# A fused two-block kernel: every matmul operand moved down by 32 bytes in SBUF

## The chip, the core and the metric

The kernel runs on one NeuronCore of a Trainium2 chip. The metric is the device time of one execution in microseconds; three runs of the kernel before stand behind the median. All arithmetic is in fp32, and nearly all matmuls read their operands as fp32r.

## What is computed

The reference is two residual blocks in sequence on one sequence of 256 tokens with 1024 channels. Cut to its matmuls:

```python
# block 1
proj = rmsnorm(x) @ w_in              # q, k, v, gates of three mixers
mixed = sum(sigmoid(gate_b) * (mixer_b(proj) @ w_branch_b))   # GLA, pooling, block attention
x = x + rmsnorm(mixed @ w_out)
f = (silu(h @ ffn_w_gate) * (h @ ffn_w_up)) @ ffn_w_down      # h = rmsnorm(x)
x = x + rmsnorm(f)
# block 2: the same shape with other mixers (HGRN2, mLSTM, SSD),
# a causal convolution in the FFN and a last rmsnorm
```

All the large products have K = 1024 (or 512, or 2816) and 256 rows. To keep fp32 accuracy each is made of three fp32r products: high part by high part, low part by high part, and high part by low part.

## The kernel before

**Tiles.** The packed weights are cut into 172 pieces of up to 2144 columns. `fetch` (L422 and after) brings a piece from HBM into a raw buffer `wr` on SP's queue, ScalarE rounds it into the high part `wh` (`act`, L283), and VectorE makes the low part `wl` by subtracting (`tt`, L286). There are two raw buffers and three each of `wh` and `wl`, so pieces are loaded and split ahead of the matmuls. Activations that feed matmuls are split in the same way, into `hhi`/`hlo` (the normed input) or into pairs of "big" buffers `b` (tag `b8`, ten of them), which also serve everything else of that size.

**Matmuls.** `three` (L445 and after) issues the products of a piece in order: all K tiles of one of the three combinations, then those of the next. There are two forms. In `proj_cm` the weights are stationary (128 columns of `wh` or `wl`) and the activations move (256 columns): the records `pp<-hhi,wh`, `pp<-hlo,wh`, `pp<-hhi,wl`, `pp<-b,wh` and `pp<-b,wl` with 128x256. In `mm_tm` (`proj_tm`, `out_tiles`, `down_tiles`, `first_tm`) the activations are stationary and the weights move, 512 columns as a rule; 256 in the first pieces of each FFN; 264 and 268 in four odd pieces whose rows in the buffer are 1056 and 1072 bytes long. All matmuls are issued by `mm`, so they share line L297; generators stepped by `tick` put the small matmuls of the mixers between the pieces.

**What lies where in a partition.** The pools are laid one behind the other: `cp` (the small constants and `x`), `wp` (`wr`, `wh`, `wl`), `pd` (a dead tile of 48 floats, 192 bytes), `big`, `hp` (`hhi`, `hlo`), `wk`. The widths of the repeated buffers are padded: `WW` = 2176 floats is 34 times 256 bytes, `BW` = 2112 floats is 33 times 256, and two `wr` of `PW` = 2144 floats are 67 times 256. So all `wh` and `wl` have one address residue modulo 256, and all big buffers and `hhi`/`hlo` have another, 192 higher. K tiles within a buffer lie 1024 or 2048 bytes apart (1056 and 1072 in the odd pieces). In the kernel before, the residues are 32 for `wh`/`wl` and 224 for the big buffers and `hhi`/`hlo`; the two `wr` are at 32 and 160.

**The lines that the change touches.** `setup` (L331 to L347) allocates `cp`'s tiles in this order: `x`, `const`, `vecs`, `wg2`, `mhalf`, `ones`, `sgain`, and last `pad`, 8 floats that nothing reads or writes. `const` holds the identity that the transposes use as the moving operand.

Of the kernel before, what the change touches and what calls it, by code (L numbers as in the profile page):

```python
# [8 lines left out]
F32 = mybir.dt.float32  # L9
# [220 lines left out]
class Prog:  # L230
# [102 lines left out]
    def setup(self):  # L333
        nc, A = self.nc, self.A
        self.x = self.cp.tile([128, 2, D], F32, name="x")
        self.const = self.cp.tile([128, CONST.shape[1]], F32, name="const")
        self.vec = self.cp.tile([128, VEC_N], F32, name="vecs")
        self.wg2 = self.cp.tile([16, 256], F32, name="wg2")
        self.mhalf = self.cp.tile([128, 16], F32, name="mhalf")
        self.warm = self.wk.tile([128, 1024], mybir.dt.bfloat16, tag="junk", name="warm", bufs=1)[:, :128]  # L340
        self.nc.vector.memset(self.warm, 0.0)
        self.nc.vector.memset(self.mhalf, -0.5)
        self.ones = self.cp.tile([128, 128], F32, name="ones")
        self.nc.vector.memset(self.ones, 1.0)
        self.sg = self.cp.tile([128, 16], F32, name="sgain")
        self.ident = self.c("ident")
        self.cp.tile([128, 8], F32, name="pad")  # L347

    def load_first(self):

# [1205 lines left out]
```

## Time and profile before

| | us |
|---|---|
| median of three runs | 1045.87 (1043.8 to 1047.94) |
| the profiled execution | 1044.58 |
| its span, first to last instruction | 1042.8 |
| TensorE busy in the span | 1028.4 (99%) |
| weight loads busy (beside the matmuls) | 963.8 (92%) |
| VectorE busy | 749.1 (72%) |
| ScalarE busy | 602.6 (58%) |

[...]

### The profile page before, as it was taken

How to read it: one execution, taken by the hardware profiler on the slowest of the kernel's cores; microseconds unless marked ns; L12 is line 12 of the kernel's file. 1: busy time of each engine (PE TensorE's matmuls, PEld its weight loads, DVE VectorE, ACT ScalarE, POOL GpSimd, SP SyncE). 2: the span in 40 equal slices, each digit the busy share in tenths (PEclk: the TensorE clock that was granted, in tenths of full speed). 3: DMA queues.
4: the chain of work that ended last, by engine and by line, in shares of the span. 5: the costliest groups of instructions: out<-in, count | busy, mean ns of one | idle time of the engine just before them, and what ended most of it. 6: DMA issues, size and time to landing. Idle time of an engine off the chain costs nothing.

```text
span 1042.8 us, 21285 instructions
## 1 busy us (share of the span) xinstructions
PE 1028.4 (99%) x8748; PEld 963.8 (92%) x8748; DVE 749.1 (72%) x1469; ACT 602.6 (58%) x1262; POOL 31.1 (3%) x53
## 2 busy tenths in 40 slices
PE   8999999999999999999999999999999999999997
PEld 7899999989999988799889899999999989999885
DVE  5767578586555645756888879877776785999753
ACT  6667555466544544744468656754565565767542
POOL 1000000000000000000020000000100000000000
PEclk9999999999999999999999999999999999999999
DMA  8654445555555556355435455455646464555561
GB/s 303 214 202 134 160 160 175 200 195 202 203 170 203 194 182 218 133 201 200 146 131 204 133 186 178 167 189 185 217 162 212 173 221 163 190 192 189 183 212 46
DMA packets 31345, 191.09 MB, mean 183 GB/s; under 512 B 3880, under 2 KB 5216, under 8 KB 10256
## 3 DMA queue, kind: packets, MB, share of 16 engines
q1 hardware_dynamic: 28544, 181.12, 49.9%
q0 software_dynamic: 2128, 7.57, 2.3%
q8 instruction: 68, 1.11, 0.4%
q10 hardware_dynamic: 576, 1.05, 0.3%
q14 instruction: 29, 0.24, 0.1%
HBM read 188.65 MB, written 1.08 MB: 182 GB/s over the span
## 4 chain that ended last, share of the span: by engine, by line
PE 95%; DVE 2%; ACT 1%; issue 1%; DMA 0%; POOL 0%; POOLq 0%; SPq 0%; ACTq 0%
PE pp L297 88%; PE m L297 5%; PE m L548 1%; DMA vecs<-vec 0%; PE m L615 0%; DVE wl L286 0%; DVE b L286 0%; ACT wh L283 0%; PE m L990 0%; PE m L814 0%; DVE k L289 0%; POOL k L567 0%; ACT hhi L283 0%; ACT b L283 0%; PE m L1321 0%
## 5 line engine op out<-in xcount | busy, mean ns | idle before, releaser
L286 DVE TENSOR_TENSOR wl<-wr,wh 128x512 fp32r<-128x512 f32 (+2 forms) x660 | 423.7, 681 | 174.7 <-ACT wh L283 91.1
L283 ACT ACTIVATE wh<-wr 128x512 fp32r<-128x512 f32 (+2 forms) x660 | 373.1, 618 | 281.1 <-PE pp L297 247.9
L297 PE MATMUL pp<-hhi,wh 128*128 128x256 f32 x1440 | 200.1, 280 | 1.1 <-ACT hhi L283 1.1
L297 PE MATMUL pp<-hlo,wh 128*128 128x256 f32 x1440 | 194.2, 277 | 0.0
L297 PE MATMUL pp<-hhi,wl 128*128 128x256 f32 x1440 | 193.8, 277 | 0.0
L297 PEld LDWEIGHTS pp<-hhi,wh 128*128 128x128 f32 x1440 | 179.8, 188 | 4.0 <-ACT hhi L283 2.1
L297 PEld LDWEIGHTS pp<-hlo,wh 128*128 128x128 f32 x1440 | 177.8, 188 | 0.0
L297 PEld LDWEIGHTS pp<-hhi,wl 128*128 128x128 f32 x1440 | 177.7, 188 | 0.0
L297 PE MATMUL pp<-wh,b 128*128 128x512 f32 x512 | 131.6, 397 | 1.7 <-ACT wh L283 1.7
L297 PEld LDWEIGHTS pp<-wh,b 128*128 128x128 f32 x512 | 97.0, 191 | 23.6 <-ACT wh L283 2.0
L297 PE MATMUL pp<-b,wh 128*128 128x256 f32 x576 | 74.6, 279 | 0.0
L289 DVE SCALAR_TENSOR_TENSOR k<-pp,vecs,k 128x255 f32<-128x255 f32 (+1 forms) x148 | 70.2, 478 | 6.1 <-ACT k L283 5.2
L297 PE MATMUL pp<-wl,b 128*128 128x512 f32 x256 | 71.4, 396 | 0.0
L297 PEld LDWEIGHTS pp<-b,wh 128*128 128x128 f32 x576 | 69.5, 188 | 0.1
L297 PEld LDWEIGHTS pp<-wl,b 128*128 128x128 f32 x256 | 48.7, 190 | 10.6
L297 PE MATMUL pp<-wh,hhi 128*128 128x512 f32 (+3 forms) x232 | 52.2, 355 | 0.0
L297 PE MATMUL pp<-wh,hlo 128*128 128x512 f32 (+3 forms) x232 | 50.2, 347 | 0.2 <-issue 0.2
L297 PE MATMUL pp<-wl,hhi 128*128 128x512 f32 (+3 forms) x232 | 50.3, 347 | 0.0
L283 ACT ACTIVATE k<-pp,vecs 128x256 f32<-128x256 f32 x62 | 34.5, 558 | 15.8 <-DVE k L289 11.3
L297 PEld LDWEIGHTS pp<-wh,hlo 128*128 128x128 f32 x232 | 38.0, 188 | 6.0 <-issue 0.3
L283 ACT ACTIVATE k<-k 128x512 f32<-128x512 f32 (+2 forms) x47 | 27.0, 574 | 28.4 <-DVE k L289 23.7
L297 PEld LDWEIGHTS pp<-wl,hhi 128*128 128x128 f32 x232 | 37.9, 188 | 5.6
(178 smaller groups left out, 929.6 us busy)
## 6 DMA issues: line engine op xcount, KB each, us to landing
wr<-w SPq DMA_DIRECT2D x158, 1024.0 KB, 4.8
wr<-w SPq DMA_DIRECT2D x10, 512.0 KB, 4.2
k<-rows POOLq DMA_DIRECT2D x16, 192.0 KB, 3.4
wr<-w SPq DMA_DIRECT2D x10, 256.0 KB, 4.4
wr<-w SPq DMA_DIRECT2D x2, 1072.0 KB, 4.9
wr<-w SPq DMA_DIRECT2D x2, 1056.0 KB, 5.1
b<-gains POOLq DMA_DIRECT2D x2, 1024.0 KB, 6.5
b<-xt SPq DMA_DIRECT2D x8, 128.0 KB, 4.5
```

The lines of the kernel that those rows point to most:

```text
L283: return self.nc.scalar.activation(out=out, in_=in_, func=func, **k)
L286: return self.nc.vector.tensor_tensor(out=out, in0=a, in1=b, op=op)
L289: return self.nc.vector.scalar_tensor_tensor(out=out, in0=a, scalar=s, in1=b, op0=op0, op1=op1)
L297: return self.nc.tensor.matmul(out, lhsT=lhsT, rhs=rhs, start=start, stop=stop)
L548: self.nc.tensor.transpose(ps[:, k], part[:, 128 * k:128 * k + 128], self.ident)
```

## The change

One allocation is dropped, the unused tile `pad` of 32 bytes a partition:

```diff
         self.sg = self.cp.tile([128, 16], F32, name="sgain")
         self.ident = self.c("ident")
-        self.cp.tile([128, 8], F32, name="pad")
```

Everything allocated ahead of it (`x`, `const`, `vecs`, `wg2`, `mhalf`, `ones`, `sgain`) stays where it is. Everything behind it moves down by 32 bytes: the weight buffers go from residue 32 to 0 modulo 256, the big buffers and `hhi`/`hlo` from 224 to 192, the raw buffers from 32 and 160 to 0 and 128, and the work tiles with them. The distance between any two of these stays the same. No instruction is added, removed or reordered.

## Rows read from the trace of the kernel before

**Rows 1.** The page: the span, busy time by engine, and the clock row.

```profile
span 1042.8 us, 21285 instructions
PE 1028.4 (99%) x8748; PEld 963.8 (92%) x8748; DVE 749.1 (72%) x1469; ACT 602.6 (58%) x1262; POOL 31.1 (3%) x53
PEclk9999999999999999999999999999999999999999
```

**Rows 2.** The page: the chain that ended last, by engine.

```profile
PE 95%; DVE 2%; ACT 1%; issue 1%; DMA 0%; POOL 0%; POOLq 0%; SPq 0%; ACTq 0%
```

**Rows 3.** Groups by line and form on TensorE: xcount | busy us, mean ns.

```profile
L297 PE MATMUL pp<-hhi,wh 128*128 128x256 f32 x1440 | 200.1, 280 | 1.1 <-ACT hhi L283 1.1
...
L297 PE MATMUL pp<-b,wh 128*128 128x256 f32 x576 | 74.6, 279 | 0.0
...
L297 PE MATMUL pp<-b,wl 128*128 128x256 f32 x288 | 40.8, 277 | 0.0
```

**Rows 4.** TensorE's timeline, weights stationary, fast: start us, us, what; first and last.

```profile
40.02 1.07 PE L297 MATMUL pp<-hhi,wl 128*128 128x256 f32 x8
...
971.73 1.07 PE L297 MATMUL pp<-hhi,wl 128*128 128x256 f32 x8
...
974.45 1.07 PE L297 MATMUL pp<-hhi,wl 128*128 128x256 f32 x8
```

**Rows 5.** The same view and shape, slow stretches: the first and the last.

```profile
71.28 1.10 PE L297 MATMUL pp<-hlo,wh 128*128 128x256 f32 x8
...
75.05 1.10 PE L297 MATMUL pp<-hhi,wl 128*128 128x256 f32 x8
...
777.47 1.11 PE L297 MATMUL pp<-b,wl 128*128 128x256 f32 x8
```

**Rows 6.** Stretches: PE, PEld, DVE, ACT, POOL busy us, clock, DMA share; two slow, one fast.

```profile
71.30:75.90 4.60, 4.60 (x42) 4.60 (x40) 1.35 (x3) 1.51 (x5) 0.00 (x0) 1.00 0.56 183
110.00:114.90 4.90, 4.90 (x44) 4.90 (x44) 4.13 (x17) 2.58 (x10) 0.00 (x0) 1.00 0.01 3
...
692.30:697.50 5.20, 5.20 (x48) 5.20 (x47) 3.26 (x6) 1.97 (x5) 0.00 (x0) 1.00 0.53 180
```

**Rows 7.** TensorE's timeline: a piece with rows of 1056 bytes, weights moving.

```profile
65.59 1.13 PE L297 MATMUL pp<-wl,hhi 128*128 128x264 f32 x8
66.56 1.13 PE L297 MATMUL pp<-wh,hhi 128*128 128x264 f32 x8
```

**Rows 8.** TensorE's timeline: the first FFN's first pieces, 256 columns moving.

```profile
238.85 1.12 PE L297 MATMUL pp<-b,hlo 128*128 128x256 f32 x8
239.81 2.08 PE L297 MATMUL pp<-b,hhi 128*128 128x256 f32 x16
...
244.81 1.10 PE L297 MATMUL pp<-wh,hlo 128*128 128x256 f32 x8
245.75 1.11 PE L297 MATMUL pp<-wl,hhi 128*128 128x256 f32 x8
```

**Rows 9.** Groups by line and form on TensorE: 512 columns moving, from `wh`, from `b`.

```profile
L297 PE MATMUL pp<-wh,hhi 128*128 128x512 f32 x136 | 38.0, 400 | 0.0
...
L297 PE MATMUL pp<-b,hhi 128*128 128x512 f32 x16 | 4.4, 398 | 0.0
```

**Rows 10.** Groups by line and form on ScalarE and VectorE: the splits.

```profile
L283 ACT ACTIVATE wh<-wr 128x512 fp32r<-128x512 f32 x628 | 358.6, 623 | 260.9 <-PE pp L297 232.2 <-DMA wr<-w 21.2 <-issue 6.1
...
L283 ACT ACTIVATE b<-wr 128x512 fp32r<-128x512 f32 x28 | 15.5, 620 | 7.8 <-DMA wr<-w 7.8
...
L286 DVE TENSOR_TENSOR wl<-wr,wh 128x512 fp32r<-128x512 f32 x628 | 407.5, 687 | 154.8 <-PE pp L297 82.1 <-ACT wh L283 71.2 <-issue 0.4
...
L286 DVE TENSOR_TENSOR b<-wr,b 128x512 fp32r<-128x512 f32 x28 | 17.8, 687 | 6.8 <-ACT b L283 6.8
```

**Rows 11.** Groups by line and form on TensorE: transposes, identity moving.

```profile
L548 PE MATMUL m<-const,b 128*128 128x128 f32 x56 | 7.4, 272 | 0.0
...
L990 PE MATMUL m<-const,k 128*128 128x128 f32 x24 | 4.6, 271 | 0.0
```

## The prediction

> **What bounds the kernel now.** First the busy table and the clock: TensorE is busy 1028.4 of 1042.8 us at the full granted clock throughout [rows 1]. Then the chain that ended last: 95% of it is TensorE [rows 2], and the rest lies mostly at the start and the end. So the time is the sum over 8748 matmuls of what each costs in the stream. Next, which matmuls: 1440 each of `hhi,wh`, `hlo,wh` and `hhi,wl`, 576 of `b,wh` and 288 of `b,wl` have stationary weights and 256 moving columns, 5184 or six in ten [rows 3]; the first row there stands for its three.
>
> Last the timeline, where the finding is. Twenty-four such matmuls go from 971.73 to 974.45, 2.72 us or 113.3 ns each [rows 4]. Elsewhere thirty-two of the same shape on the same kinds of buffer go from 71.28 to 75.05, 3.77 us or 117.8 ns each [rows 5]. Counted from start to start over the whole trace, for steps between two matmuls of this form without a gap, 4042 take 113 to 116 ns (mean 113.4) and 1035 take 117 to 124 (mean 117.9); the first and the last rows of either kind stand in [rows 4, 5]. They aren't mixed: a stretch, usually the 48 matmuls of a piece, keeps one rhythm from its first few matmuls to its end. The rhythm does not follow the other engines: one slow stretch has the DMA engines 56% busy and VectorE 29%, another has DMA at 1% and VectorE at 84%, a fast one lies between with 53% and 63%, all at clock 1.00 and with the weight loads busy all the time [rows 6]. So TensorE is held back by something of its own. Two reads of SBUF run in it at once, the moving operand of one matmul and the weights of the next, and I take it that they collide, in a pattern that depends on their addresses and on how the stretch was entered.
>
> **The trace's own evidence on addresses.** The odd pieces keep the stationary operand at residue 224 while the moving one advances by 32 modulo 256 from one matmul to the next, so eight matmuls visit eight places. Eight take 0.97 us, 121.2 ns each at 264 columns [rows 7]; counted from start to start the mean is 121.0, in a settled cycle of 116 to 126 ns with the same time at the same place each round. [...] Two further pairings stand in the FFN's first pieces: both operands at residue 224, 0.96 us for eight, 120 ns; stationary 224 and moving 32, 0.94 us, 117.5 ns by the row and 118.0 by the count [rows 8]. Of all pairings that whole stretches have, that of the bulk, stationary 32 and moving 224, is the only one with a rhythm near 113.
>
> **The change, part by part.**
> *The 5184 matmuls with stationary weights.* Their operands go to residues 0 and 192, a pair that the trace does not hold. Is it the place or the distance that counts? The distance stays at 192. [...] If the place counts, the expectation is the mean over places, 117.7 [rows 7], not the best: 4042 x (117.7 - 113.4) = 17.4 us more, and 1035 x (117.9 - 117.7) = 0.2 less, together 17 us. Bounds: all at the worst settled pairing, 120 [rows 8], 4042 x 6.6 + 1035 x 2.1 = 28.9 us more; all at the best place seen, 112.7, 4042 x 0.7 + 1035 x 5.2 = 8.2 us less. I take 17, by the row with eight places in steps of the very 32 bytes.
> *The matmuls with 512 moving columns*, 1248 by the count: moving from `wh` at 32 or from `b` at 224 past the same stationary 224, the records last 400 and 398 ns [rows 9]. They hardly see the address; I take 0, bounded by 2 ns either way, 2.5 us.
> *The other forms with 256 to 268 moving columns and stationary activations*, 480 by the count: they already sit at the slow rhythm or above, so 0, bounded by 480 x 5 = 2.4 us, likelier as a gain than as a loss.
> *The transposes*, 174: here alone the distance changes, since the identity stays. The stationary operand lies at 224 in one row and at 32 in the other, 272 against 271 ns [rows 11]: 174 x 1 ns = 0.2 us, nothing.
> *The splits on ScalarE and VectorE* write `wh`/`wl` at residue 32 and `b` at 224 in the same 623 and 620 ns, and in the same 687 and 687 ns [rows 10]. Their addresses cost nothing there, so 0. The cover, if I am wrong, is that ScalarE mostly waits for TensorE, 232.2 us of the 260.9 idle ahead of its splits; 3 ns on 656 splits is 2 us of that, and without the cover it would be 2 us.
> *The loads* into `wr` land at other residues. ScalarE's splits waited only 21.2 us for them in the whole run [rows 10], nearly all behind pieces already split, so a faster landing is worth nothing and a slower one is covered by the buffers ahead; 0, with 0.5 us either way at the start, where the chain isn't on TensorE.
>
> Sum, against the profiled execution: 1044.6 + 17 = 1061.6, so 1062 us. Outside the span lie 1.8 us that don't change. This execution is 1.3 us under the median of the three, inside their spread of 4.1. The measurement can tell 0.5%, 5.2 us, from no change.
>
> **Rivals.**
> *A, the forecast: the place counts and the fast rhythm is lost*, 1062 us. For it: the fast rhythm stands alone among the pairings of whole stretches. [...] Its own range is 1050 (a third of the stretches still fast, -5.8 us, and some 6 us of gain at the other forms and bounds) to 1076 (28.9 + 2.5 over 1044.6).
> *B, only the distance counts*, 1045 us. Where the two reads meet depends on one address less the other if the memory repeats in steps of 32 bytes or less, and a shift of both changes nothing. For it: the weight buffers, which lie 512 apart modulo 1024, and both halves of a piece show the same 113.4, so the pattern does repeat. What can still move is how the stretches fall into the two rhythms: the longest, one in each FFN, are 860 matmuls each, so one of them entered the other way is 860 x 4.5 = 3.9 us. That alone is nearly the spread of the runs. Range 1040 to 1051.
> [...]
> *C, the new places are better*: every stretch finds the fast rhythm or a better one. The slow rhythm disappears, 1035 x 4.5 = 4.7 us, and with the best place seen it is 8.2 us, plus up to 2.4 at the other forms. 1044.6 - 6.5, the middle of the first two, is 1038 us, range 1034 to 1040. [...]
> *D, the change doesn't do what it says*, because the allocator puts the buffers elsewhere: the pools are laid in order and the tile has no reader, so this is unlikely; 1045 us as B.
>
> **How the numbers follow.** A 0.45, B 0.31, C 0.22, D 0.02. [...] The predicted time is A's, 1062. The range leaves out half of C (below 1038) and the top of A (above 1075), about 0.16: 1038 to 1075. Faster by over 0.5%: C less a little, plus a little of B, 0.22. Slower: A less a little that stays within 5 us, plus a little of B, 0.44. Within: 0.34.
>
> **What the new profile would show.** If A: in the timeline of the stationary-weight stretches eight take 0.94 to 0.96 us where most now take 0.907, the recorded mean of these groups rises from 277 to about 281 ns, and the FFN stretches of 860 are slow throughout; VectorE's and ScalarE's splits stay at 687 and 623. If B: the same two steps, 0.907 and 0.945, in shares near four to one. If C: a single step of 0.907 or less. The prediction is wrong if the 512-column stream moves by more than 2 ns a matmul, or if the splits' durations change; then the reading that only TensorE's own two reads see the address fails.

## The result

| | before | after |
|---|---|---|
| median of four runs, us | 1044.84 (1043.36 to 1047.94) | 1054.27 (1051.73 to 1055.52) |
| profiled execution, us | 1044.58 | 1054.15 |
| its span, us | 1042.8 | 1052.3 |
| ratio, with its 95% interval | | 1.0085 (1.0067 to 1.0103) |

The change makes the kernel 0.85% slower, 9.4 us. The page of the kernel after, the lines that answer to [rows 1]:

```profile
span 1052.3 us, 21285 instructions
PE 1036.2 (98%) x8748; PEld 972.5 (92%) x8748; DVE 748.1 (71%) x1469; ACT 602.0 (57%) x1262; POOL 31.1 (3%) x53
PEclk9999999999999999999999999999999999999999
```

TensorE has the same 8748 matmuls and is busy 7.8 us longer; VectorE and ScalarE need no more than before. Where, the chain that ended last tells, in order of time: start us, us, what. First three of its longest pieces in the kernel before, then the same three after:

```profile
263.38 151.51 PE pp L297 x1098
...
785.79 62.83 PE pp L297 x468
...
877.58 151.51 PE pp L297 x1098
```

```profile
261.01 155.35 PE pp L297 x1098
...
789.83 64.50 PE pp L297 x468
883.29 155.35 PE pp L297 x1098
```

3.84 + 1.67 + 3.84 = 9.35 us of the 9.5 us by which the spans differ, in three stretches. In each the part that changed is a run of matmuls with stationary weights: 863 steps, from one start to the next, in either FFN, and 383 in eight pieces at the end of block 2's branches (at 785 us). Outside the three, the two executions differ by -2.4 us ahead of the first stretch and by +2.6 between the first and the second, which nearly cancels. That is luck of the two profiles. The first 30 us took longer in this profile of the kernel before than in any other profile here, by 1.1 to 2.5 us. The +2.6 are mostly a wait and a spell of lower clock near 530 and 548 us of the kernel after, which the profile of before does not have there:

```profile
532.29 0.52 PE L297 MATMUL pp<-hlo,wh 128*128 128x256 f32 x3 [1.33 <-issue]
...
547.00:550.40 3.40, 3.40 (x40) 0.53 0.68 219
```

The first line is from the timeline, with an idle time of 1.33 us in square brackets; the second is a stretch, in which the granted clock was 0.53, against 1.00 in the same window of the kernel before. A kernel without the loss has the wait too (1.35 us, with the work tiles put back, below), and a kernel with the loss has no such spell of lower clock there (the unused bytes first, below), so neither is the change's loss.

The timeline of TensorE shows how one of them begins, first before, then after. Columns as in [rows 4]; L990 before and L989 after are the same line, the last two transposes ahead of the first FFN's stretch.

```profile
263.00 0.38 PE L990 MATMUL m<-const,k 128*128 128x128 f32 x2
263.13 1.17 PE L297 MATMUL pp<-hhi,wh 128*128 128x256 f32 x8
264.14 1.07 PE L297 MATMUL pp<-hlo,wh 128*128 128x256 f32 x8
265.05 1.07 PE L297 MATMUL pp<-hhi,wl 128*128 128x256 f32 x8
```

```profile
260.62 0.38 PE L989 MATMUL m<-const,k 128*128 128x128 f32 x2
260.76 1.19 PE L297 MATMUL pp<-hhi,wh 128*128 128x256 f32 x8
261.79 1.11 PE L297 MATMUL pp<-hlo,wh 128*128 128x256 f32 x8
262.73 1.11 PE L297 MATMUL pp<-hhi,wl 128*128 128x256 f32 x8
```

The records of neighbouring matmuls overlap: eight last 1.07 us before and 1.11 after, while the next eight start 0.91 and 0.94 us on. So the time of one is taken here from the starts, the step to the next row divided by eight. Eight matmuls take 0.91 us before and 0.94 after, the very two rhythms of [rows 4] and [rows 5], and the difference is there from the second group of eight on. It lasts to the end of the stretch. The view by stretches, with the matmuls that start in the same 96.8, 43.0 and 97.0 us, before and then after. (The kernel after enters its second and third stretch 3.6 and 5.1 us into these windows, so a few other matmuls are counted there.)

```profile
263.20:360.00 96.80, 96.80 (x856) 1.00 0.55 191
786.00:829.00 43.00, 43.00 (x382) 1.00 0.57 203
878.00:975.00 97.00, 97.00 (x858) 1.00 0.55 188
```

```profile
263.20:360.00 96.80, 96.80 (x824) 1.00 0.54 185
786.00:829.00 43.00, 43.00 (x369) 1.00 0.53 184
878.00:975.00 97.00, 97.00 (x828) 1.00 0.52 180
```

In these windows TensorE is busy all the time, at clock 1.00, and gets through 32, 13 and 30 fewer matmuls.

**No rhythm changed its length.** Counted from the starts, past the first steps of a stretch, the fast rhythm is 113.33 ns and the slow one 117.78 in the long stretches of both kernels, to the hundredth (with the entry, a whole fast FFN stretch has 113.35). What changed is the share over the whole trace: 1035 of 5077 steps are slow before, 3184 of 5066 after. The matmuls outside this form kept their times: 117.9 ns (stationary 224 or 192, moving 32 or 0), 121.0 at 264 columns, 123.9 and 124.1 at 268, 229.2 and 229.2 at 512. So moving all operands by 32 bytes changed nothing where both operands of a matmul moved.

### The profile page after: what moved, and what is told of

It reads as the page before. It is cut to its first block, busy times and chain, and to the rows that moved or that the text cites. A ratio compares the mean times of both kernels' runs of the same rounds, so it can differ in the third digit from the quotient of the medians.

```text
span 1052.3 us, 21285 instructions
## 1 busy us (share of the span) xinstructions
PE 1036.2 (98%) x8748; PEld 972.5 (92%) x8748; DVE 748.1 (71%) x1469; ACT 602.0 (57%) x1262; POOL 31.1 (3%) x53
## 3 DMA queue, kind: packets, MB, share of 16 engines
q8 instruction: 68, 1.11, 0.4%
## 4 chain that ended last, share of the span: by engine, by line
PE 94%; DVE 2%; DMA 1%; ACT 1%; issue 1%; POOL 0%; SPq 0%; POOLq 0%; ACTq 0%
PE pp L297 87%; PE m L297 5%; DMA wr<-w 1%; PE m L547 1%; DMA x<-x 1%; PE m L614 0%; DVE wl L286 0%; DVE b L286 0%; POOL k L566 0%; ACT junk L561 0%; ACT wh L283 0%; PE m L989 0%; PE m L813 0%; DVE k L289 0%; ACT b L283 0%
## 5 line engine op out<-in xcount | busy, mean ns | idle before, releaser
L297 PE MATMUL pp<-hhi,wh 128*128 128x256 f32 x1440 | 203.0, 282 | 1.1 <-ACT hhi L283 1.1
L297 PE MATMUL pp<-hlo,wh 128*128 128x256 f32 x1440 | 198.2, 280 | 1.3 <-issue 1.3
L297 PE MATMUL pp<-hhi,wl 128*128 128x256 f32 x1440 | 197.0, 280 | 0.0
L297 PEld LDWEIGHTS pp<-hhi,wh 128*128 128x128 f32 x1440 | 182.2, 189 | 4.0 <-ACT hhi L283 2.1
L297 PEld LDWEIGHTS pp<-hlo,wh 128*128 128x128 f32 x1440 | 181.4, 189 | 1.5 <-issue 1.4
L297 PEld LDWEIGHTS pp<-hhi,wl 128*128 128x128 f32 x1440 | 180.9, 189 | 0.0
```

The costliest lines, as they stand in the source:

```text
L297: return self.nc.tensor.matmul(out, lhsT=lhsT, rhs=rhs, start=start, stop=stop)
```

## The experiments

After the result the theories were these. **E**: the length of a rhythm is set by the distance of the two operands; which rhythm a stretch falls into is set by how it is entered, that is by what TensorE read just before, and there the identity of the transposes is an operand that did not move. **P**: the place modulo 256 of weights and activations makes the slow rhythm likelier. **X**: the entry falls by chance.

### The kernel before, a second profile

No edit.

> The kernel before, unchanged, profiled a second time. In the first profiles of before and after, each long stretch of matmuls with stationary weights keeps one of two rhythms, 113.3 or 118 ns a matmul; three long stretches (860, 860 and 382 matmuls, entered near 263, 877 and 786 us) are fast before and slow after, and they are worth 9.7 us. Theory E (the entry is set by program and addresses: the transposes just ahead read the identity, which the change did not move): all three are fast again, near 1044 us. Theory X (the entry falls by chance, and the two profiles happened to differ): one or more of the three are slow here, 2 to 10 us more in the span. Theory P (the place of the weights modulo 256 makes the slow rhythm likelier): as E.

Measured: 1043.3 us, span 1041.5. The stretches of 863, 383 and 863 have 113.35, 113.36 and 113.35 ns, as in the first profile. Of the 53 stretches some short ones, and one of 183 steps, fall otherwise than in the first profile, 1277 slow steps against 1035, which is 1.1 us. So chance has a small share and not the three long stretches. The times of all executions say the same: all four of the kernel after took 1051.7 us or more, and none of 17 of the kernel before took more than 1047.7. X falls for these.

### The unused bytes ahead of `x` and `const`

```diff
+        self.cp.tile([128, 8], F32, name="pad")
         self.x = self.cp.tile([128, 2, D], F32, name="x")
         self.const = self.cp.tile([128, CONST.shape[1]], F32, name="const")
...
-        self.cp.tile([128, 8], F32, name="pad")
```

> Before, with the unused 32 bytes allocated ahead of x and const instead of behind them: the weights stay at residue 32 and the big buffers at 224, as before, but the identity moves up by 32, so its distance to everything behind is that of the changed kernel. Theory E (what counts is the distance between the identity and the tiles that the transposes ahead of a stretch turn): the three long stretches are slow, ratio 1.008 to 1.010, about 1054 us. Theory P (the place of the weights and activations modulo 256 counts): as before, ratio 1.000 within 0.2%. Theory X (chance): no fixed answer.

Measured: 1055.93 us, ratio 1.0105 (1.0087 to 1.0123). All three long stretches are slow, 117.78 ns. The entry of the second FFN's, from this kernel's timeline:

```profile
883.34 0.38 PE L990 MATMUL m<-const,k 128*128 128x128 f32 x2
883.48 1.19 PE L297 MATMUL pp<-hhi,wh 128*128 128x256 f32 x8
884.50 1.11 PE L297 MATMUL pp<-hlo,wh 128*128 128x256 f32 x8
885.45 1.10 PE L297 MATMUL pp<-hhi,wl 128*128 128x256 f32 x8
```

Here not one weight or split activation lies elsewhere than before; only `x` and the small constants ahead of them moved. Of these TensorE reads, beside the identity, only `ones` and `wg2`, in eight matmuls that all lie in the first 80 us. The slowdown of the change is there in full, so the place of the weights is not its cause. P falls.

### The identity moved along

The changed kernel, with small tiles put between `x` and `const`, so that the identity goes down by 32 modulo 256 like all the rest.

```diff
         self.x = self.cp.tile([128, 2, D], F32, name="x")
+        self.mhalf = self.cp.tile([128, 16], F32, name="mhalf")
+        self.sg = self.cp.tile([128, 16], F32, name="sgain")
+        self.r0 = [self.cp.tile([128, 1], F32, name=f"r0_{t}") for t in range(2)]
+        self.ml_gain = self.cp.tile([128, 8], F32, name="mlg")
         self.const = self.cp.tile([128, CONST.shape[1]], F32, name="const")
```

> The changed kernel with 224 bytes of small tiles (mhalf, sgain, the two r0 and mlg) allocated between x and const instead of behind, so that the identity too goes down by 32 modulo 256, from 128 to 96, with the weights at 0 and the big buffers at 192. All distances modulo 256 among the operands of the large matmuls and the transposes are those of before. Theory E: the three long stretches are fast, ratio 1.000 within 0.2%, about 1045 us. Theory P: slow as after, 1.008 to 1.010, about 1054 us.

Measured: 1045.15 us, ratio 1.0009 (0.9993 to 1.0025). The three stretches are fast, and with the weights at 0 and the activations at 192 the time of before is back. Timeline at the entry of the stretch of 383:

```profile
782.92 1.04 PE L549 MATMUL m<-const,b 128*128 128x128 f32 x8
783.71 1.17 PE L297 MATMUL pp<-hhi,wh 128*128 128x256 f32 x8
784.72 1.07 PE L297 MATMUL pp<-hlo,wh 128*128 128x256 f32 x8
785.62 1.07 PE L297 MATMUL pp<-hhi,wl 128*128 128x256 f32 x8
```

These two runs and the two kernels make a square: weights at the old or the new place, identity at the old or the new distance. The time follows the distance of the identity in both rows.

### Only the work tiles back

The changed kernel with 32 unused bytes at the head of the work pool, which puts the work tiles, and they alone, back where they were before.

```diff
+        self.wk.tile([128, 8], F32, tag="padk", name="padk", bufs=1)
         self.nc.vector.memset(self.warm, 0.0)
```

> The changed kernel with 32 unused bytes put into the work pool, so that the work tiles alone go back to their places of before (the 256-column ones to residue 160) while weights, big buffers and normed input stay at 0 and 192 and the identity at 128. The transposes that turn a work tile (line 990, just ahead of the two FFN stretches of 860, and line 814) have their distance of before again; those that turn a big buffer (lines 548, 615, 1321, ahead of the stretch of 382 near 786 us and the one of 285 near 182 us) keep that of the changed kernel. Theory E: the two FFN stretches are fast, the stretch of 382 stays slow: 8.0 us less than the changed kernel, about 1046.3, ratio 1.002. Rival P': it is the shift of the FFN's own operands, weights and normed input, that makes their stretches slow: no gain, 1054, ratio 1.009.

Measured: 1043.74 us, ratio 1.0003 (0.9992 to 1.0013). The two FFN stretches are fast, as E said and P' denied. But the stretch of 383 is fast too, which E's account had slow: its last transposes turn a big buffer and kept the distance of the changed kernel. So the last transposes alone don't decide there. The edit moved the work tiles against the big buffers as well, and these meet in the small matmuls of the SSD that run among the pieces just ahead: the five stretches of 48 to 96 matmuls that are entered from such a matmul (716 to 778 us) are slow in both kernels and fast here. The traces show one thing more that differs, the rhythm of the piece ahead of the last transposes. The timeline around the last eight, first of the kernel after, then of this run:

```profile
786.07 1.98 PE L297 MATMUL pp<-b,wh 128*128 128x256 f32 x16
787.88 1.07 PE L297 MATMUL pp<-b,wl 128*128 128x256 f32 x8
788.79 1.04 PE L547 MATMUL m<-const,b 128*128 128x128 f32 x8
...
790.61 1.11 PE L297 MATMUL pp<-hlo,wh 128*128 128x256 f32 x8
791.55 1.10 PE L297 MATMUL pp<-hhi,wl 128*128 128x256 f32 x8
```

```profile
778.52 2.05 PE L297 MATMUL pp<-b,wh 128*128 128x256 f32 x16
780.40 1.11 PE L297 MATMUL pp<-b,wl 128*128 128x256 f32 x8
781.34 1.04 PE L548 MATMUL m<-const,b 128*128 128x128 f32 x8
...
783.15 1.07 PE L297 MATMUL pp<-hlo,wh 128*128 128x256 f32 x8
784.05 1.07 PE L297 MATMUL pp<-hhi,wl 128*128 128x256 f32 x8
```

The same eight transposes at the same distance stand between: in the kernel after a fast piece is followed by a slow stretch, here a slow piece (117.8 ns) by a fast one. As far as these two kernels show it, the outcome depends on the rhythm that comes in as well as on the distance of the transposes, so the chain may well reach back to the SSD's matmuls. In all seven profiles with the bulk at distance 192 the three long stretches are slow exactly where the work tiles no longer have before's distance from the identity.

By the count this run has 431 slow steps, 604 fewer than before, which should be worth 2.7 us. Its profiled span, 1039.4, is 3.4 us under that of before, but 2.0 of these fall in the first 30 us, and of the 2.7 a wait of 1.35 us near 525 us takes half. Its median does not show the gain, and the interval allows 0.8 us at most. Why, is open.

### The identity 64 bytes further

The kernel before, with `mhalf` (64 bytes) allocated ahead of `const` instead of behind.

> Before, with one tile of 64 bytes (mhalf) allocated ahead of const instead of behind, so the identity is at 192 and all else that the large matmuls read stays where it was before. Theory E: stretches entered from something other than a transpose (near 447, 731, 767 us) keep their rhythm of before; of those entered from a transpose some change, and which way can't be told: all fast gives 0 to 1 us less than before, the three long ones slow 9.7 us more; 1043 to 1054. A rival by which the identity matters only at the distance of the changed kernel, not in general, gives 1044.5.

Measured: 1056.02 us, span 1054.2. The three long stretches are slow (117.78 ns), and the matmuls with 512 columns run slower in part, 231.2 ns in the mean against 229.2, which is 2.4 us more. Besides, the granted clock was 0.52 for 3.4 us near 35 us of this execution, which the profile of before does not have. Together they take the time past the 1054 that was expected at most. The identity's new distance is neither that of before nor that of after. So the distance of after has nothing special; an identity elsewhere can send the same stretches into the slow rhythm. The other stretch of 383, entered near 450 us from a 512-column matmul, is slow in both profiles of before and in that of after, and fast here (113.39) as it is with the identity moved along and with the work tiles back. E had it keep its rhythm, since no transpose stands directly ahead of it; that part of E failed, and what decides there is open.

### Other distances between weights and activations

The dead tile between the weight buffers and the big buffers was given other widths, which moves all activations against all weights. Each kernel is the one before, but for that of 224, which is the changed one.

```diff
-        e(tc.tile_pool(name="pd", bufs=1)).tile([128, 48], F32, name="padw")
+        e(tc.tile_pool(name="pd", bufs=1)).tile([128, 32], F32, name="padw")
```

> Before, with 32 instead of 48 floats in the dead tile between the weight buffers and the big buffers: the distance from weights to activations is 128 modulo 256 instead of 192, weights stay at 32, big buffers go to 160. In the odd pieces with rows of 1056 bytes the place at this distance had the shortest time, 116 ns for 264 columns. Theory E in its general form (two reads of TensorE meet in a pattern set by their distance): both forms of matmul now lie at 128; if the odd pieces' place is a guide, 112.7 ns in one rhythm for the stationary weights, ratio 0.99; if a settled rhythm differs from a passing one, anything from 113 to 120 ns, ratio 0.99 to 1.035. The 512-column matmuls change too, by up to 5 ns, 6 us. Theory P has no forecast but that the weights' place is unchanged, so about 1.000.

> Before, with 40 instead of 48 floats between weight and big buffers: distance 160 instead of 192, weights at 32. Theory E: other distances have other rhythms; the odd piece's place at this distance gave 119 ns for 264 columns, 115.7 for 256, but the run at 128 showed that such a place is no guide, so 113 to 120 ns: 1040 to 1075 us, and a repeating pattern of few lengths again. A theory without distance gives 1044.5.

> The changed kernel (weights at 0) with 56 instead of 48 floats between weight and big buffers: distance 224 instead of 192. Theory E: as for 160, 113 to 120 ns a matmul with stationary weights, 1040 to 1075 us; the odd pieces' worst place (126 ns for 264 columns) had this distance. A theory without distance gives the changed kernel's 1054.

> Before, with 24 instead of 48 floats between weight and big buffers: distance 96 instead of 192, weights at 32. So far distance 192 had 113.3 or 118 ns a matmul with stationary weights, 128, 160 and 224 had 118.3 to 118.8 in the mean, 0 had 120. Theory E: another repeating pattern; if 192 is the exception, a mean of 117 to 120, 1060 to 1073 us; if distances in the lower half are good, 113 and below, 1030 to 1040 us.

> Before, with 8 instead of 48 floats between weight and big buffers: distance 32 instead of 192, weights at 32. Theory E: as for 96; 1060 to 1073 us if 192 is the exception, 1030 to 1040 us if not.

> Before, with 16 instead of 48 floats between weight and big buffers: distance 64 instead of 192 for stationary weights, and 192 for moving weights. Moving weights past stationary activations had the distance 64 so far and took 117.9 ns at 256 columns. If only the distance of the moving from the stationary operand counts, the stationary-weight form takes about 118 here, 1065 us, and the 256-column pieces with moving weights get 113.3 or 118. If the role of the weights counts as well, other lengths.

> Before, without the dead tile between weight and big buffers: all operands at residue 32, distance 0. In the pieces whose both operands lie in big buffers distance 0 gives 120.0 ns, with no second rhythm. If only the distance counts, 120 here, 5100 x (120.0 - 114.3) = 29 us more, 1073.

Measured, with the mean time from start to start of the matmuls with stationary weights (256 columns, some 5070 steps) and of those with 512 moving columns:

| distance, activations less weights | us | mean, 256 columns, ns | in the FFN stretches of 863, ns | 512 columns, ns |
|---|---|---|---|---|
| 0 | 1068.57 | 119.9 | 120.0 | 227.3 |
| 32 | 1060.15 | 116.8 | 116.67 | 233.1 |
| 64 | 1056.69 | 115.9 | 113.33 | 233.1 |
| 96 | 1078.19 | 120.0 | 119.99 | 233.9 |
| 128 | 1070.48, ratio 1.0242 (1.0219 to 1.0265) | 118.8 | 118.67 | 232.3 |
| 160 | 1069.41 | 118.6 | 120.0 | 233.2 |
| 192 (before) | 1044.84 | 114.3 | 113.35 | 229.2 |
| 224 | 1072.04 | 118.3 | 118.33 | 233.1 |

All but those of 128 and 192 rest on one execution each, and such a time carries 1 or 2 us of the start and of short spells of lower clock; the nanoseconds are counted without these. A 512-column matmul has the weights moving, so its moving operand lies at the same distance the other way round from the stationary one. Two neighbouring groups of eight from the timelines of 160 and of 32, in the first FFN:

```profile
300.10 1.12 PE L297 MATMUL pp<-hhi,wl 128*128 128x256 f32 x8
301.06 1.12 PE L297 MATMUL pp<-hhi,wh 128*128 128x256 f32 x8
```

```profile
300.21 1.10 PE L297 MATMUL pp<-hlo,wh 128*128 128x256 f32 x8
301.15 1.10 PE L297 MATMUL pp<-hhi,wl 128*128 128x256 f32 x8
```

0.96 us for eight at 160, 0.94 at 32. The lengths go with the distance, as E had it: at 32 the steps run 113, 116, 118, 120 and again, at 128 they run 115, 118, 122, 120, 119, at 160 there is an even 120 in the FFN stretches and a longer pattern of 115 to 120, 117.3 in the mean, in the stretches of 383, at 64 the same two rhythms of 113.3 and 117.8 as at 192. The forecast for 128 from the odd piece, 112.7 and a ratio of 0.99, was wrong: the odd piece has 116 ns for 264 columns at the place that it passes once in eight matmuls, and the streams that stay there took 118.8 in the mean for 256. For 64 the forecast of about 118 from the FFN's first pieces held for only part of the stretches; those pieces are 24 matmuls long, and all of them had entered the slow rhythm. The pieces with 256 moving weight columns, which lie at 192 in that run, did take both 113.3 and 118, 115.6 in the mean. The forecast for 0, 120 ns, held (the time was 4 us under the forecast, the 512-column form having gained 2 ns on 1248 matmuls, 2.4 us). None of the eight distances beats the one that the kernel has.

## Why the prediction was right in its bounds and wrong in its reason

The time of 1054 lies in the stated range, but no rival had priced what came: it is between A's 1062, whose rhythm did not come, and the top of B's range, 1051. That the range holds it is owed to its width, which was made from the spread of A and C, and so to luck.

*What bounds the kernel, the two rhythms, and that other engines have no part in them*: right. The loss of the three stretches is TensorE's, where it is busy throughout at clock 1.00, and VectorE's and ScalarE's work did not grow (749.1 to 748.1 and 602.6 to 602.0 us).

*The stationary-weight matmuls*, +17 us: the step failed at its first question, "Is it the place or the distance that counts?" I took the place, and gave A more than B. The odd piece's place at the same distance of 192, 122 to 123 ns at 264 columns, was no evidence for that: each matmul there follows one at another distance. The mean over eight places, 117.7, is my estimate for 256 columns from the 121.0 ns counted at 264, and no run shows it. The same goes for the 112.7 behind the bound of 8.2 us and the forecast for 128, and for the 115.7 in the forecast for 160. What the runs showed in place of 117.7: the matmuls kept both their rhythms to the hundredth of a nanosecond, 113.33 and 117.78. The 17 us are about twice the 9.4 measured, since I moved all 4042 fast steps by 4.3 ns, where 2149 more steps turned slow by 4.43 ns: 9.5 us.

*Rival B, only the distance counts*: right for each matmul by itself, and its time, 1045, was wrong. It named the way in which the loss came, "one of them entered the other way is 860 x 4.5 = 3.9 us" (3.84 was measured), and allowed for that as scatter. It came as a fixed effect, in three long stretches at once. *Rival C*, every stretch fast, failed with A: the slow rhythm gained 2149 steps, and none shorter than the fast one appeared.

*The transposes*, "here alone the distance changes, since the identity stays", priced at 0.2 us and "nothing": this is the term that was missing. Their own time did change by no more than that. (The tiles that L990 turns lie at 160, as the expectation of the run with the work tiles back has it, and not at 32, as the prediction reads them; the price hardly depends on it.) By the records' starts the last two ahead of the first FFN take 109 and 26 ns before, 110 and 28 after. With the identity at that distance the stretch behind them falls into the slow rhythm, and there it costs 3.84 us. That these 3 ns are what shifts it is not shown: with the work tiles back the last two ahead of the second FFN take 110 and 27 ns, and that stretch is fast. I priced an operation by its own duration, having found that a stretch's rhythm depends on its entry; the two findings were not put together.

*Splits, loads, 512-column matmuls and other forms at nothing*: right here. The reason given for the 512-column form, that it hardly sees the address, is not: over the eight distances it takes 227.3 to 233.9 ns, and it kept its time, 229.2 ns, where its distance stayed. Groups by line and form of the kernel after, columns as in [rows 3] and [rows 10]:

```profile
L297 PE MATMUL pp<-hlo,wh 128*128 128x256 f32 x1440 | 198.2, 280 | 1.3 <-issue 1.3
...
L297 PE MATMUL pp<-wh,hhi 128*128 128x512 f32 x136 | 38.0, 400 | 0.0
...
L283 ACT ACTIVATE wh<-wr 128x512 fp32r<-128x512 f32 x628 | 358.5, 622 | 274.0 <-PE pp L297 252.3 <-DMA wr<-w 18.4 <-issue 1.9
...
L286 DVE TENSOR_TENSOR wl<-wr,wh 128x512 fp32r<-128x512 f32 x628 | 406.3, 685 | 164.8 <-PE pp L297 87.1 <-ACT wh L283 76.3 <-issue 0.2
```

The splits read 622 and 685 ns for the former 623 and 687, and the 512-column form of [rows 9] 400 again. ScalarE's wait for TensorE rose from 232.2 to 252.3 us, the loss seen from behind.

*The signs named for A* came true in part only: the FFN stretches are slow throughout, and the recorded mean of the groups of [rows 3] rose, to 280 from 277 in the second and third. But these were also the signs of B with the entries turned, and the two steps of 0.907 and 0.945, named for B, were both still there. What told the two apart was a sign that I had not named: whether the forms outside the bulk kept their times.

What stays open: how far back the state at the entry reaches (the run with the work tiles put back shows that it is more than the last transposes); what decides at the stretch near 450 us; and what inside TensorE or SBUF makes the pattern, which no run here looked into. The trace shows the weight loads beside the matmuls, 188 ns in the mean, in streams with steps of 113.3 or 117.8; that the moving operand's read and the next weights' read collide is argued from the dependence on their distance, not shown.

## What to carry to other kernels

Where TensorE is busy throughout, read the starts of equal matmuls and not their durations: here one shape had two settled rhythms, 113.3 and 117.8 ns, and TensorE was busy 99% of the span with 1035 slow steps and 98% with 3184. If a change moves addresses, ask for every pair of operands whether their distance changes, and count an operation just ahead of a long stretch by the rhythm of the stretch behind it (3.84 us in the first FFN), not by its own nanoseconds (110 and 28). Before a gain or loss of a per cent is put down to an edit's purpose, compare where the long stretches fell.

## What the runs showed of the hardware

The time of a stream of 128x128 weights and 256 moving fp32r columns goes with the distance modulo 256 between its two operands, 113.3 to 120.0 ns in the long stretches, and not with where the pair lies (32 and 224 against 0 and 192, ratio 1.0009 with the identity moved along; both operands at 224, 120 ns [rows 8], against both at 32, 119.9). At the distances 64 and 192 there are two rhythms, 113.3 and 117.8; at 192 each was kept for 863 steps. At 192 the address distance between the operands of a few transposes ahead, and the rhythm of the piece before these, went with one or the other (117.78 ns in the three long stretches with the identity 32 bytes further, 0.91 us for eight with it moved along, and with the work tiles back 113.3 behind a piece of 117.8). The distance that is best for 256 columns with stationary weights (192, 114.3 ns) isn't the best for 512 columns (0, 227.3 against 229.2 ns).
